# PSUM banks for the meta rows and the value bounds in the late in-projection jobs of a hybrid attention layer

## The chip, the cores and the metric

The kernel runs on one core of one Trainium2 chip. The metric is the device time of one execution, in microseconds (us), as the median of several runs.

## What is computed

One decoder layer. 16 learned meta tokens stand ahead of 1024 tokens of width 1024; everything is float32.

```
proj = rmsnorm(x) @ w_in      # c_q 256 | c_kv 128, k_r 32 | q_s 512 | k_s 512 | v_s 512 | indexer
o_mla = causal_block_attention(q_mla, k_mla, v_mla)     # q, k, v from rmsnorm(c_q) @ w_uq, rmsnorm(c_kv) @ w_ukv
score = where(causal, sum_h w_i * relu(q_i . k_i), -inf)
sel   = top_k(score, 256)                               # per query
o_dsa = softmax attention of rope(q_s) over rope(k_s)[sel], v_s[sel]
x = x + concat(o_mla, o_dsa) @ w_o
x = x + swiglu(rmsnorm(x)); out = rmsnorm(x), meta rows dropped
```

## The kernel before

**Products.** A float32 product is made of three products of split operands (`three`, L189 to L191: high by high, low by high, high by low). The sequence is cut into eight blocks t = 0..7 of 128 tokens (`NB`); the 16 meta rows stand apart, as `um`, with high and low part side by side, so that their products (`proj_m`, L307 and L308) are two and not three per slice of the contraction. The contraction has eight slices (`ND`).

**In-projection.** Its columns are cut into seven jobs (`run(i)`). A job loads its weights (`wraw`), splits them (`wh` by ACT at L181, `wl`), and makes for every block t a PSUM tile of 24 products, which `job` takes away (evacuates): the queries and keys of attention B through the ACT copy `st` (L516), the rotation on DVE (`rq`, L327 to L329) and a DMA to DRAM (`ks_x<-st`); the values by `v_parts`, an ACT product `vs` (L170) and a DVE one (L171), both scaled by `vsc`. After block t = 5 (`M_AT`) of a late job, `job_m` makes the meta rows; ACT copies their low half to `mlo` (L310) and DVE adds the high half to it (L311). Jobs 0 to 2 are the early ones (`EARLY`), and of the late ones job 3 (320 columns) holds queries and keys, job 4 keys, and jobs 5 and 6 values (256 columns each).

**The value bound.** Ahead of the tiles of jobs 5 and 6, `v_bound` bounds the values: ACT makes eight tiles `aw` = |wh| times the norm's gain (L574, two buffers), PE adds them up by products with ones (L575), and `v_scale` turns the sum into the power of two `vsc` on DVE (`vw`, L161 to L166). `mla_weights`, after job 3, has a bound of the same kind for attention A's values.

**What runs between.** `fill` puts steps of the top-k search for attention B's blocks between the tiles: on DVE a search round over two blocks' scores (L390, L390, L397, L398, L399, sixteen rounds) and after it the ranking of ties (L438 to L451), on ACT a search round over one block (`js` L375, then L376 and L378). After job 6 the parts of attention A follow (from L695), then attention B, the output projection and the FFN.

**Banks and order.** PSUM has eight banks, each a tile name `b0` to `b7` with one buffer. A ring is a string of bank digits taken in turn; a tile that gets a bank must wait until the last reader of that bank's earlier tile is done. Before the change the late jobs' blocks take the ring `ps_j` = 0,5,1,6,2,7,3, their meta rows the ring `ps_p` = 0,1,2, and the three bounds `ps_t` = 3,4. The program is written in the order of these loops; then a scheduler moves instructions within each engine's queue by its own timeline, and on the chip every engine runs its queue strictly in order.

Of the kernel before, what the change touches and what calls it, by code (L numbers as in the profile page):

```python
# [49 lines left out]
FILL = 1  # L50


PSI = "012", "34", "567", "0516273"
PSA = "01", "2345", "67"
PSB = "01", "2", "3", "4", "5", "67"
PSW = "45", "67", "23", "01"
# [3 lines left out]
EARLY, MLA_W, M_AT, XT_G, W_ENGS = 3, 3, 5, 2, "g"  # L60
# [38 lines left out]
def hybrid_layer(ctx, tc, a, out):  # L99
# [57 lines left out]
    def v_scale(pool, i, bound, rest):  # L157


        w = pool.tile([P, 4], F32, name="vw")  # L160
        V.reduce_max(w[:, 0:1], bound, axis=AX.X)  # L161
        V.tensor_scalar(w[:, 0:1], w[:, 0:1], 1e-25, None, op0=OP.max)
        wi, vi = w.bitcast(I32), vsc[i].bitcast(I32)
        V.tensor_scalar(wi[:, 1:2], wi[:, 0:1], 0x7F800000, None, op0=OP.bitwise_and)
        V.tensor_scalar(vi[:, 0:1], wi[:, 1:2], -1.0, float((268 - rest) << 23), op0=OP.mult, op1=OP.add)
        V.tensor_scalar(vi[:, 1:2], wi[:, 1:2], float((rest - 14) * (1 << 23)), None, op0=OP.add)  # L166

    def v_parts(h, l, src, i):
        n = src.shape[0]
        S.activation(h, src, AF.Copy, scale=vsc[i][:n, 0:1])  # L170
        V.scalar_tensor_tensor(l, src, vsc[i][:n, 0:1], h, op0=OP.mult, op1=OP.subtract)  # L171
# [23 lines left out]
    def ring(banks):  # L195

        turn = itertools.cycle(banks)
        return lambda: pp.tile([P, 512], F32, name=f"b{next(turn)}", bufs=1)
# [32 lines left out]


    with ExitStack() as es:
        ps_p, ps_t, ps_l, ps_j = (ring(x) for x in PSI)

        up = es.enter_context(tc.tile_pool(name="up", bufs=1))
        uH = up.tile([P, ND, T], F32R, name="uH")
# [11 lines left out]
        def load_chunk(c0, w, engs):  # L249

            res = []
            for d in range(ND):
                raw = wp.tile([P, 328], F32, name="wraw", bufs=3)
                ld(raw[:, :w], a["w_in"][0, d * P:(d + 1) * P, c0:c0 + w])
                h = wp.tile([P, 328], F32R, name="wh", bufs=2 * ND)
                l = wp.tile([P, 328], F32R, name="wl", bufs=2 * ND)
                split(h[:, :w], l[:, :w], raw[:, :w], engs[d % len(engs)])
                res.append((h, l))
            return res
# [39 lines left out]
                h, l = ws[d]  # L299
                three(o, uH[:, d, sl], uL[:, d, sl], h[:, :w], l[:, :w], d == 0, d == ND - 1)  # L300

        def proj_m(ws, w):

            o = ps_p()
            for d in range(ND):
                h, l = ws[d]
                PE.matmul(o[0:64, :w], um[:, d, :], h[:, :w], start=d == 0, stop=False)  # L307
                PE.matmul(o[0:64, :w], um[:, d, :], l[:, :w], start=False, stop=d == ND - 1)  # L308
            lo = ip.tile([NM, 328], F32, name="mlo", bufs=1)
            S.activation(lo[:, :w], o[32:32 + NM, :w], AF.Copy)  # L310
            V.tensor_add(lo[:, :w], o[0:NM, :w], lo[:, :w])  # L311
            return lo

        def rope(outs, src, cs, sn, shape, tag, eng=G, eng1=V):

            hf = shape[-1] // 2
            parts = shape[0]
            t1 = ip.tile([P] + list(shape[1:]), F32, name=tag + "1", bufs=2)[:parts]
            t2 = ip.tile([P] + list(shape[1:]), F32, name=tag + "2", bufs=2)[:parts]

            def bc(x):
                for _ in shape[1:-1]:
                    x = x[:, None]
                return x

            sh = list(shape[:-1]) + [hf]
            eng1.tensor_mul(t1, src, bc(cs).to_broadcast(list(shape)))  # L327
            V.tensor_mul(t2[..., 0:hf], src[..., hf:2 * hf], bc(sn[:, 0:hf]).to_broadcast(sh))
            V.tensor_mul(t2[..., hf:2 * hf], src[..., 0:hf], bc(sn[:, hf:2 * hf]).to_broadcast(sh))  # L329
            for o in outs:  # L330
                eng.tensor_add(o, t1, t2)
# [141 lines left out]
        m = proj_m(wk, 328)  # L473
# [33 lines left out]
        def latent(dst, src, n, g, parts=P):  # L507
            ss = ip.tile([P, 1], F32, name="ssc", bufs=3)[:parts]
            S.activation(act_junk()[:parts, :n], src, AF.Square, accum_out=ss)
            r = rstd(ip, ss, n, parts, "rsc")  # L510
            V.scalar_tensor_tensor(dst, src, r, g[:parts], op0=OP.mult, op1=OP.mult)

        def roped_heads(dx, rows, h0, src, cs, sn, scale=1.0, parts=P):
            n = src.shape[-1] // HD
            st = ip.tile([P, 5, HD], F32, name="st", bufs=3)[:parts, :n]
            S.activation(st, src.rearrange("p (h d) -> p h d", d=HD), AF.Copy, scale=scale)  # L516
            rope([st], st, cs, sn, [parts, n, HD], "rq")
            for i in range(2):
                ld(dx[rows, h0:h0 + n, i], st)

        def heads_of(c0, w):

            nq = max(0, min(w, O_KS - c0))
            res = [(0, (c0 - O_QS) // HD, nq, -HD ** -0.5)] if nq else []
            return res + ([(nq, (c0 + nq - O_KS) // HD, w - nq, 1.0)] if nq < w else [])
# [24 lines left out]
                if t == NB - 1:  # L550
                    ld(v_x[1][:, 4 * g:4 * g + 4, :, 1:], vs)

        def job_m(c0, w, ws):
            if c0 < O_CKV or O_CKV < c0 < O_KS - 64:
                return
            m = proj_m(ws, w)
            if c0 == O_CKV:
                latent(cm[:, 0:KVR], m[:, 0:KVR], KVR, gq[:, QR:], NM)
                rope([cm[:, KVR:160]], m[:, KVR:160], ropem[:, 128:160], ropem[:, 160:192], [NM, RD], "rr", V)
            elif c0 < O_VS:  # L560
                c, h, n, _ = heads_of(c0, w)[-1]
                roped_heads(ks_m, slice(0, NM), h, m[:, c:c + n], ropem[:, 0:64], ropem[:, 64:128], 1.0, NM)
            else:
                g = (c0 - O_VS) // 256
                mv = vsp.tile([NM, 4, 2, HD], F16, name="mv")
                v_parts(mv[:, :, 0], mv[:, :, 1], m[:, :w].rearrange("p (h d) -> p h d", d=HD), 1 + g)
                ld(v_x[1][PAD:, 4 * g:4 * g + 4, :, 0], mv)

        def v_bound(c0, w, ws):

            pb = ps_t()
            for d, (h, _) in enumerate(ws):
                aw = vsp.tile([P, 256], F32R, name="aw", bufs=2)
                S.activation(aw[:, :w], h[:, :w], AF.Abs, scale=gcol[:, d:d + 1])  # L574
                PE.matmul(pb[:, :w], ones, aw[:, :w], start=d == 0, stop=d == ND - 1)  # L575
            v_scale(vsp, 1 + (c0 - O_VS) // 256, pb[:, :w], 5)
# [4 lines left out]
        def run(i):  # L581
            c0, w = jobs[i]
            ws = nxt.pop()
            if i + 1 < len(jobs):
                nxt.append(load_chunk(*jobs[i + 1], ENG_W))
            if c0 >= O_VS:
                v_bound(c0, w, ws)
            for t in range(NB):
                po = (ps_p if i < EARLY else ps_j)()
                proj(po[:, :w], t, ws, w)  # L590
                job(c0, w, t, po)
                fill(FILL)
                if t == (NB - 1 if i < EARLY else M_AT):
                    job_m(c0, w, ws)

        flush()
        for i in range(EARLY):
            run(i)
# [21 lines left out]
        def mla_weights():  # L620
            def v8(t):
                return t.rearrange("p (h d) -> p h d", h=8)

            def raw(src):
                x = wp.tile([P, 328], F32, name="wraw", bufs=3)
                ld(x[:, 0:256], src)
                return x[:, 0:256]

            for c in range(4):
                x = raw(a["w_ukv"][0, :, c * 256:(c + 1) * 256]).rearrange("p (h t d) -> p h t d", h=2, t=2)  # L630
                hs = slice(2 * c, 2 * c + 2)
                split(v8(wkH)[:, hs], v8(wkL)[:, hs], x[:, :, 0], G)
                split(v8(wvH)[:, hs], v8(wvL)[:, hs], x[:, :, 1], G)
            for k in range(2):
                for c in range(3):
                    cs = slice(c * 256, (c + 1) * 256)
                    split(wqH[:, k, cs], wqL[:, k, cs], raw(a["w_uq"][0, k * P:(k + 1) * P, cs]), G)
            pb = ps_t()
            for c in range(2):
                cs = slice(c * 256, (c + 1) * 256)  # L640
                aw = vsp.tile([P, 256], F32R, name="aw", bufs=2)
                S.activation(aw, wvH[:, cs], AF.Abs, scale=gcol[:, ND:])
                PE.matmul(pb[:, cs], ones, aw, start=True, stop=True)
            v_scale(vsp, 0, pb, 4)
# [18 lines left out]
    ps_s, ps_t, ps_o = (ring(x) for x in PSA)  # L663
# [513 lines left out]
    ps_s, ps_t, ps_o, ps_g, ps_u, ps_y = (ring(x) for x in PSB)  # L1177
# [75 lines left out]
```

## Time and profile before

| | |
|---|---|
| median of 3 runs | 1524.23 us (1519.41 to 1525.39) |
| profiled execution | 1528.41 us, its span 1526.6 us |
| mean granted TensorE clock | 0.981 of full speed |
| busy share of the span | PE 94%, PE weight load 87%, DVE 59%, ACT 55%, POOL 52% |

The shares are means over the whole span. Times below are positions in the span of the profiled execution, which is 0.27% longer than the median; the late jobs lie between about 200 and 327 us.

### The profile page before, as it was taken

To read this page: it belongs to the slowest core of one execution; us is meant where nothing else is said; L and a number is where in the kernel's file an instruction comes from. 1 tells how busy PE (TensorE), PEld (TensorE's weight loads), DVE (VectorE), ACT (ScalarE), POOL (GpSimd) and SP (SyncE) were. 2 spreads that over 40 slices of the span, in tenths; PEclk is the share of its full clock that TensorE was granted. 3 is DMA by queue.
4 is the path that set the end of the run, shared out by engine and by line. 5 is a ranking of instruction groups with operands and counts; after the bars stand their busy time and mean duration, and the time that the engine had idled before them with its cause. 6 is when DMAs were issued, how large, how long until landed. Compare 5 with 4: busy or idle time off the path is not lost. (4 is left out here: it accounts for less than half of the span.)

```text
span 1526.6 us, 29766 instructions
## 1 busy us (share of the span) xinstructions
PE 1434.4 (94%) x10584; PEld 1332.2 (87%) x10584; DVE 907.2 (59%) x2447; ACT 846.6 (55%) x2038; POOL 796.2 (52%) x1121
## 2 busy tenths in 40 slices
PE   6999998999989899899899999999999999999997
PEld 5999998888778788788798899888899999999996
DVE  6879989948886876966866666415422222213225
ACT  5666678797889889797544453435412122122223
POOL 2663555212405678786887888531634344343342
PEclk9999999999999799999999999999999999999999
DMA  6123355224434787587799997431322222222221
GB/s 180 50 52 85 86 136 125 47 88 143 125 103 107 163 187 171 138 182 148 177 212 200 204 210 172 138 108 39 125 82 84 67 85 65 74 83 70 83 70 69
DMA packets 353732, 180.71 MB, mean 118 GB/s; under 512 B 196560, under 2 KB 341344, under 8 KB 353584
## 3 DMA queue, kind: packets, MB, share of 16 engines
q1 hardware_dynamic: 353584, 178.82, 46.7%
q8 instruction: 83, 1.36, 0.4%
q14 instruction: 65, 0.53, 0.1%
HBM read 120.77 MB, written 21.30 MB: 93 GB/s over the span
## 5 line engine op out<-in xcount | busy, mean ns | idle before, releaser
L184 POOL TENSOR_TENSOR wL<-raw,wH 128x256 fp32r<-128x256 f32 x528 | 399.1, 787 | 303.0 <-ACT wH L181 293.3
L181 ACT ACTIVATE wH<-raw 128x1024 fp32r<-128x1024 f32 x132 | 139.7, 1058 | 263.2 <-PE b L191 96.4
L189 PE MATMUL b<-ub,wH 128*128 128x384 f32 (+1 forms) x704 | 218.6, 311 | 1.2 <-ACT wH L181 1.2
L190 PE MATMUL b<-ub,wH 128*128 128x384 f32 (+1 forms) x704 | 218.5, 311 | 0.0
L191 PE MATMUL b<-ub,wL 128*128 128x384 f32 (+1 forms) x704 | 217.8, 310 | 0.0
L814 POOL TENSOR_TENSOR hl<-pd,hl 128x260 f16<-128x260 f32 (+5 forms) x256 | 168.4, 686 | 72.6 <-ACT hl L810 39.6
L189 PE MATMUL b<-wh,uH 128*128 128x256 f32 (+3 forms) x568 | 169.1, 298 | 5.3 <-DVE mlo L311 2.6
L191 PE MATMUL b<-wh,uL 128*128 128x256 f32 (+3 forms) x568 | 168.5, 297 | 0.0
L190 PE MATMUL b<-wl,uH 128*128 128x256 f32 (+3 forms) x568 | 168.1, 296 | 0.1
L1107 DVE TENSOR_TENSOR oh<-b,oh 128x512 f32<-128x512 f32 x146 | 99.2, 686 | 74.5 <-PE b L191 74.1
L189 PE MATMUL b<-wH,hH 128*128 128x512 f32 x352 | 140.5, 399 | 1.8 <-DVE oh L1107 0.8
L190 PE MATMUL b<-wL,hH 128*128 128x512 f32 x352 | 138.7, 394 | 0.0
L191 PE MATMUL b<-wH,hL 128*128 128x512 f32 x352 | 136.0, 393 | 0.4 <-DVE hL L186 0.4
L189 PEld LDWEIGHTS b<-ub,wH 128*128 128x128 f32 x704 | 132.8, 189 | 3.1 <-ACT wH L181 1.5
L190 PEld LDWEIGHTS b<-ub,wH 128*128 128x128 f32 x704 | 132.2, 188 | 1.2
L191 PEld LDWEIGHTS b<-ub,wL 128*128 128x128 f32 x704 | 132.1, 188 | 1.1
L189 PE MATMUL b<-ua,wH 128*128 128x384 f32 x352 | 122.0, 347 | 4.0 <-ACT wH L181 4.0
L375 ACT ACTIVATE js<-sc,bs 128x528 bf16<-128x528 int16 (+7 forms) x128 | 120.8, 944 | 4.1 <-DVE sc L430 1.7
L191 PE MATMUL b<-ua,wL 128*128 128x384 f32 x352 | 121.0, 344 | 0.0
L190 PE MATMUL b<-ua,wH 128*128 128x384 f32 x352 | 120.9, 343 | 0.0
L1093 DVE SCALAR_TENSOR_TENSOR sg<-sg,b 128x384 f32<-128x384 f32 x66 | 33.5, 508 | 144.5 <-ACT sg L1092 144.5
L189 PEld LDWEIGHTS b<-wh,uH 128*128 128x128 f32 x568 | 108.6, 191 | 7.4 <-DVE mlo L311 3.4
(326 smaller groups left out, 4026.6 us busy)
## 6 DMA issues: line engine op xcount, KB each, us to landing
raw<-in_w_gate SPq DMA_DIRECT2D x44, 512.0 KB, 4.1
raw<-in_w_up SPq DMA_DIRECT2D x44, 512.0 KB, 4.0
raw<-in_w_down SPq DMA_DIRECT2D x44, 512.0 KB, 3.6
wor<-in_w_o SPq DMA_DIRECT2D x64, 128.0 KB, 2.6
wraw<-in_w_in SPq DMA_DIRECT2D x40, 128.0 KB, 2.3
vh<-v_x SPq DMA_DIRECT2D x16, 288.0 KB, 3.8
xt<-in_x SPq DMA_DIRECT2D x8, 512.0 KB, 4.3
ks_x<-st SPq DMA_DIRECT2D x32, 128.0 KB, 2.2
```

The costliest lines, as they stand in the source:

```text
L181: S.activation(h, src, AF.Copy)
L184: G.tensor_sub(l[:, c], src[:, c], h[:, c])
L189: PE.matmul(o, lh, rh, start=first, stop=False)
L190: PE.matmul(o, lh, rl, start=False, stop=False)
L191: PE.matmul(o, ll, rh, start=False, stop=last)
L375: S.activation(act_junk()[:, :n_keys(b)], y[b], AF.Sign, bias=cols[0], accum_out=cnt)
L814: G.tensor_sub(pl_[:, c], pb[:, c], ph[:, c])
L1093: V.scalar_tensor_tensor(sg, sg, 1.0, pg, op0=OP.add, op1=OP.mult)
L1107: V.tensor_add(oh[t][:, cs], po, oh[t][:, cs])
```

## The change

Late jobs now take their meta rows' bank from the same ring as their blocks, as one more slot between t = 5 and t = 6. All three bounds take a ring of their own with the single bank 4, which in this stage only `ps_t` holds besides.

```
-PSI = "012", "34", "567", "0516273"
+PSI = "012", "34", "567", "0516273", "4"
...
-        ps_p, ps_t, ps_l, ps_j = (ring(x) for x in PSI)
+        ps_p, ps_t, ps_l, ps_j, ps_b = (ring(x) for x in PSI)
...
-        def proj_m(ws, w):
+        def proj_m(ws, w, ps=ps_p):
 
-            o = ps_p()
+            o = ps()
...
         def v_bound(c0, w, ws):
 
-            pb = ps_t()
+            pb = ps_b()
...
+            ps = ps_p if i < EARLY else ps_j
             for t in range(NB):
-                po = (ps_p if i < EARLY else ps_j)()
+                po = ps()
...
-                    job_m(c0, w, ws)
+                    job_m(c0, w, ws, ps)
...
-            pb = ps_t()              # in mla_weights
+            pb = ps_b()
```

No engine gets an instruction more or less. The banks of the late jobs become these (blocks t = 0 to 5, then meta rows m, then t = 6, 7):

| job | before | after |
|---|---|---|
| 3 | 0 5 1 6 2 7, m 2, 3 0 | 0 5 1 6 2 7, m 3, 0 5 |
| 4 | 5 1 6 2 7 3, m 0, 0 5 | 1 6 2 7 3 0, m 5, 1 6 |
| 5 | bound 3; 1 6 2 7 3 0, m 1, 5 1 | bound 4; 2 7 3 0 5 1, m 6, 2 7 |
| 6 | bound 4; 6 2 7 3 0 5, m 2, 1 6 | bound 4; 3 0 5 1 6 2, m 7, 3 0 |

The scheduler's order changes with them, on all engines from job 3 on to the end of attention B. In the rows of the order, a name ends in the number of its buffer, and `b3_4420` is a tile in bank 3.

PE, where the meta rows of job 3 (`3574`) begin, before; `3604` is job 3's block t = 6:

```order
L189 MATMUL b3_3604<-wh_2771,uH_109 128x320
L190 MATMUL b3_3604<-wl_2772,uH_109 128x320
L191 MATMUL b3_3604<-wh_2771,uL_110 128x320
L307 MATMUL b2_3574<-wh_2750,um_111 64x320
L308 MATMUL b2_3574<-wl_2751,um_111 64x320
```

And after, where `3507` is its block t = 5:

```order
L189 MATMUL b7_3507<-wh_2799,uH_109 128x320
L190 MATMUL b7_3507<-wl_2800,uH_109 128x320
L191 MATMUL b7_3507<-wh_2799,uL_110 128x320
L308 MATMUL b3_3574<-wl_2751,um_111 64x320
L307 MATMUL b3_3574<-wh_2757,um_111 64x320
```

The meta rows moved ahead of block 6: before they stand behind its 24 products.

PE, around the bound of job 5 (`4420`), before; `4311` is job 4's block 7, `4250` its block 6, and `4451` and `4505` are job 5's blocks 0 and 1:

```order
L190 MATMUL b5_4311<-wl_3153,uH_109 128x256
L191 MATMUL b5_4311<-wh_3152,uL_110 128x256
L575 MATMUL b3_4420<-aw_4421,ones_83 128x256
L575 MATMUL b3_4420<-aw_4424,ones_83 128x256
L189 MATMUL b1_4451<-wh_3806,uH_109 128x256
...
L190 MATMUL b0_4250<-wl_3153,uH_109 128x256
L191 MATMUL b0_4250<-wh_3152,uL_110 128x256
L575 MATMUL b3_4420<-aw_4427,ones_83 128x256
L189 MATMUL b1_4451<-wh_3812,uH_109 128x256
L190 MATMUL b1_4451<-wl_3813,uH_109 128x256
L575 MATMUL b3_4420<-aw_4430,ones_83 128x256
L191 MATMUL b1_4451<-wh_3812,uL_110 128x256
```

And after:

```order
L190 MATMUL b6_4311<-wl_3153,uH_109 128x256
L191 MATMUL b6_4311<-wh_3152,uL_110 128x256
L575 MATMUL b4_4420<-aw_4421,ones_83 128x256
L575 MATMUL b4_4420<-aw_4424,ones_83 128x256
L189 MATMUL b2_4451<-wh_3806,uH_109 128x256
...
L190 MATMUL b2_4451<-wl_3849,uH_109 128x256
L191 MATMUL b2_4451<-wh_3848,uL_110 128x256
L189 MATMUL b7_4505<-wh_3806,uH_109 128x256
L190 MATMUL b7_4505<-wl_3807,uH_109 128x256
L191 MATMUL b7_4505<-wh_3806,uL_110 128x256
L189 MATMUL b7_4505<-wh_3812,uH_109 128x256
L575 MATMUL b4_4420<-aw_4427,ones_83 128x256
```

Job 4's block 6 no longer stands behind the first two products of the bound; the third product of the bound stands behind a whole block and four products of the next one, and it waits for the third `aw`.

DVE, where the bound of job 5 is read (`vw` L161), before; `jk` with L390 is a round of the search:

```order
L390 TENSOR_SCALAR jk_4353,bs1_3201<-sc1_102,bs1_3201 128x272
L390 TENSOR_SCALAR jk_4355,bs1_3201<-sc2_103,bs1_3201 128x400
L397 TENSOR_TENSOR bs1_3201<-bs1_3201 128x2
L398 TENSOR_SCALAR bs1_3201<-bs1_3201 128x2
L161 TENSOR_REDUCE vw_4445<-b3_4420 128x1
L399 SCALAR_TENSOR_TENSOR bs1_3201<-bs1_3201 128x2
L162 TENSOR_SCALAR vw_4445<-vw_4445 128x1
L390 TENSOR_SCALAR jk_4479,bs1_3201<-sc1_102,bs1_3201 128x272
L390 TENSOR_SCALAR jk_4481,bs1_3201<-sc2_103,bs1_3201 128x400
L164 TENSOR_SCALAR vw_4445<-vw_4445 128x1
L397 TENSOR_TENSOR bs1_3201<-bs1_3201 128x2
L165 TENSOR_SCALAR vsc1_81<-vw_4445 128x1
```

And after:

```order
L390 TENSOR_SCALAR jk_4488,bs1_3201<-sc2_103,bs1_3201 128x400
L397 TENSOR_TENSOR bs1_3201<-bs1_3201 128x2
L398 TENSOR_SCALAR bs1_3201<-bs1_3201 128x2
L399 SCALAR_TENSOR_TENSOR bs1_3201<-bs1_3201 128x2
L161 TENSOR_REDUCE vw_4445<-b4_4420 128x1
L438 TENSOR_SCALAR jk_4532,bs1_3201<-sc1_102,bs1_3201 128x272
L441 TENSOR_SCALAR jk_4535<-sc1_102,bs1_3201 128x272
L162 TENSOR_SCALAR vw_4445<-vw_4445 128x1
L439 TENSOR_TENSOR bs1_3201<-bs1_3201 128x1
L442 SCALAR_TENSOR_TENSOR jk_4535<-sc1_102,bs1_3201,jk_4535 128x272
L164 TENSOR_SCALAR vw_4445<-vw_4445 128x1
L444 SCALAR_TENSOR_TENSOR jk_4536<-jk_4535 128x272
```

The rounds with `jk_4479` and `jk_4486`, which stood behind the reading of the bound, stand ahead of it, and the ranking (L438 to L444) begins ahead of `vsc1_81` (L165).

ACT, where the evacuation of job 5's blocks begins (`vs` L170), before; `js` L375 with L376 and L378 is a round of ACT's search:

```order
L378 ACTIVATE bs4_4147<-bs4_4147 128x1
L574 ACTIVATE aw_4828<-wh_4374,gcol_85 128x256
L375 ACTIVATE js_4360,bs4_4147<-sc4_105,bs4_4147 128x656
L574 ACTIVATE aw_4831<-wh_4380,gcol_85 128x256
L181 ACTIVATE wh_4416<-wraw_4414 128x256
L376 ACTIVATE bs4_4147<-bs4_4147,th4_4148 128x1
L378 ACTIVATE bs4_4147<-bs4_4147 128x1
L170 ACTIVATE vs_4476<-b1_4451,vsc1_81 128x4x64
L170 ACTIVATE vs_4476<-b6_4505,vsc1_81 128x4x64
```

And after:

```order
L376 ACTIVATE bs4_4147<-bs4_4147,th4_4148 128x1
L378 ACTIVATE bs4_4147<-bs4_4147 128x1
L574 ACTIVATE aw_4831<-wh_4380,gcol_85 128x256
L375 ACTIVATE js_4368,bs4_4147<-sc4_105,bs4_4147 128x656
L376 ACTIVATE bs4_4147<-bs4_4147,th4_4148 128x1
L378 ACTIVATE bs4_4147<-bs4_4147 128x1
L375 ACTIVATE js_4493,bs4_4147<-sc4_105,bs4_4147 128x656
L170 ACTIVATE vs_4476<-b2_4451,vsc1_81 128x4x64
L170 ACTIVATE vs_4476<-b7_4505,vsc1_81 128x4x64
```

The round `js_4368` stood behind block 0's evacuation and stands ahead of it, as does the next one's first step `js_4493`.

## Rows read from the trace of the kernel before

**Rows 1.** The profile page: busy time of each engine with its share of the span and its number of instructions, and the TensorE clock granted in 40 equal slices, in tenths of full speed (9 is 90% or more).
```profile
PE 1434.4 (94%) x10584; PEld 1332.2 (87%) x10584; DVE 907.2 (59%) x2447; ACT 846.6 (55%) x2038; POOL 796.2 (52%) x1121
...
PEclk9999999999999799999999999999999999999999
```

**Rows 2.** What PE waited for between 225 and 345 us: engine, waiting line, what it waited for; us in total, times, longest.
```profile
PE b L307 <- ACT st L516: 4.7, 1, 4.7
PE b L575 <- ACT st L516: 2.8, 1, 2.8
PE b L189 <- DVE mlo L311: 2.4, 2, 1.4
PE b L189 <- ACT cqH L181: 1.6, 1, 1.6
PE b L189 <- DVE vw L161: 1.0, 1, 1.0
```

**Rows 3.** The five bank waits on PE's timeline: start, us, engine, line, operation, out<-in, form; in brackets the idle time before it and what ended that.
```profile
233.00 0.53 PE L307 MATMUL b<-wh,um 128*64 128x320 f32 x1 [4.74 <-ACT st L516]
...
266.71 0.58 PE L575 MATMUL b<-aw,ones 128*128 128x256 f32 x1 [2.79 <-ACT st L516]
...
269.55 0.58 PE L189 MATMUL b<-wh,uH 128*128 128x256 f32 x1 [1.40 <-DVE mlo L311]
...
287.01 0.39 PE L189 MATMUL b<-wh,uH 128*128 128x256 f32 x1 [1.05 <-DVE vw L161]
...
299.83 0.38 PE L189 MATMUL b<-wh,uH 128*128 128x256 f32 x1 [1.03 <-DVE mlo L311]
```

**Rows 4.** Busy time in stretches: stretch and its length; then busy us (and instructions) of PE, PE's weight load, DVE, ACT, POOL; granted clock as a share, DMA share, GB/s.
```profile
226.00:275.00 49.00, 40.07 (x291) 38.82 (x290) 45.13 (x167) 40.18 (x126) 26.73 (x39) 0.90 0.51 119
...
275.00:302.00 27.00, 24.92 (x210) 24.51 (x209) 26.01 (x93) 21.22 (x61) 5.14 (x7) 1.00 0.18 42
...
300.00:325.00 25.00, 25.00 (x214) 25.00 (x214) 8.88 (x26) 22.95 (x63) 0.40 (x2) 1.00 0.13 44
...
302.00:340.00 38.00, 36.22 (x276) 34.85 (x275) 16.81 (x55) 35.13 (x101) 7.15 (x23) 1.00 0.28 89
...
228.00:259.00 31.00, 26.27 (x200) 25.51 (x200) 30.15 (x125) 23.90 (x76) 18.55 (x27) 0.94 0.56 132
...
263.00:302.00 39.00, 32.73 (x252) 31.82 (x252) 37.66 (x122) 31.73 (x92) 10.03 (x14) 0.91 0.23 53
...
340.00:460.00 120.00, 108.20 (x1043) 93.37 (x1042) 105.38 (x319) 96.47 (x297) 33.20 (x54) 0.99 0.40 119
...
460.00:1000.00 540.00, 506.65 (x4200) 458.76 (x4200) 362.97 (x915) 356.58 (x787) 401.62 (x565) 0.97 0.77 172
```

**Rows 5.** DVE's timeline, columns as in rows 3.
```profile
260.93 0.43 DVE L327 TENSOR_TENSOR rq<-st,rope 128x256 f32<-128x256 f32 x1 [1.35 <-ACT st L516]
...
263.12 0.76 DVE L438 TENSOR_SCALAR_CACHE_REDUCE jk<-sc,bs 128x528 bf16<-128x528 uint16 x1 [1.36 <-POOL bs L383]
...
283.05 0.50 DVE L390 TENSOR_SCALAR_CACHE_REDUCE jk<-sc,bs 128x272 bf16<-128x272 uint16 x1
...
284.74 0.50 DVE L390 TENSOR_SCALAR_CACHE_REDUCE jk<-sc,bs 128x272 bf16<-128x272 uint16 x1
...
286.55 0.41 DVE L161 TENSOR_REDUCE vw<-b 128x1 f32<-128x256 f32 x1
...
288.23 0.15 DVE L165 TENSOR_SCALAR vsc<-vw 128x1 int32<-128x1 int32 x1
...
291.63 0.49 DVE L438 TENSOR_SCALAR_CACHE_REDUCE jk<-sc,bs 128x272 bf16<-128x272 uint16 x1
...
293.67 0.50 DVE L445 SCALAR_TENSOR_TENSOR jk<-jk,bs 128x272 bf16<-128x272 f16 x1
...
301.95 0.20 DVE L451 TENSOR_TENSOR sc<-sc,cbias 128x128 bf16<-128x128 bf16 x1
```

**Rows 6.** ACT's timeline, columns as in rows 3.
```profile
237.00 0.22 ACT L516 ACTIVATE st<-b 128x64 f32<-128x64 f32 x1 [2.16 <-DMA ks_x<-st]
...
271.38 0.49 ACT L574 ACTIVATE aw<-wh,gcol 128x256 fp32r<-128x256 f32 x1
...
282.94 0.42 ACT L181 ACTIVATE wh<-wraw 128x256 fp32r<-128x256 f32 x1 [2.77 <-DMA wraw<-in_w_in]
...
288.41 0.47 ACT L170 ACTIVATE vs<-b,vsc 128x256 f16<-128x256 f32 x1 [2.09 <-DVE vsc L165]
...
293.19 0.83 ACT L375 ACTIVATE js<-sc,bs 128x656 bf16<-128x656 int16 x1
...
294.81 0.84 ACT L375 ACTIVATE js<-sc,bs 128x656 bf16<-128x656 int16 x1
...
295.65 0.45 ACT L170 ACTIVATE vs<-b,vsc 128x256 f16<-128x256 f32 x1
```

**Rows 7.** PE's timeline, the first product of attention A.
```profile
327.10 0.23 PE L695 MATMUL b<-ident,cm 16*128 16x16 f32 x1
```

**Rows 8.** What PE waited for between 340 and 1000 us: us in total, times, longest.
```profile
PE b L783 <- DVE sm L785: 12.1, 12, 3.0
```

More of the change, by code (lines that the diff above doesn't have):

```diff
@@ L551, in job, with job_m @@
                     ld(v_x[1][:, 4 * g:4 * g + 4, :, 1:], vs)
-        def job_m(c0, w, ws):
+        def job_m(c0, w, ws, ps):
             if c0 < O_CKV or O_CKV < c0 < O_KS - 64:
                 return
-            m = proj_m(ws, w)
+            m = proj_m(ws, w, ps)
             if c0 == O_CKV:
```

## The prediction

> **What bounds the kernel now.** I read the shares first, then the waits of PE in the stretch that the change touches, then who is late there.
>
> Over the whole span PE is busy 94% and no other engine is above 59%; the granted clock is full in all but one of the 40 slices [rows 1]. So a microsecond that PE stands idle is worth a microsecond, but only where nothing else sets the end of the stretch. The list of PE's waits between 225 and 345 us names the places that the change addresses [rows 2]: the meta rows of job 3 wait 4.74 us for bank 2, the bound of job 5 waits 2.79 us for bank 3 (both end with ACT's copy `st`), a block waits 1.40 us and another 1.03 us for `mlo`, that is for a bank that meta rows have taken, and one 1.05 us for `vw`, a bank that a bound has taken [rows 3]. The wait for `cqH` is not a bank and is left alone. The five are 4.74 + 2.79 + 1.40 + 1.05 + 1.03 = 11.0 us.
>
> Then the stretches, because a mean over 1526 us says little on 100 of them [rows 4]. From 226 to 275 us PE is busy 40.07 of 49 us, its weight load 38.82, ACT 40.18, and DVE 45.13. From 275 to 302 us PE has 24.92 of 27, DVE 26.01. Finer: DVE has 30.15 of 31 us between 228 and 259, and 37.66 of 39 between 263 and 302. Between them it waits twice, 1.35 us for an `st` and 1.36 us for a small step of the search on POOL [rows 5]. So in the late jobs DVE works without a break, and PE waits because banks come free as fast as ACT and DVE empty them. Banks are taken one after another, and each is given back by those two engines; a PE that waits less at one bank meets the next one that is still full. This is the reading on which my forecast rests.
>
> From 302 us on it turns: DVE has 16.81 us of work in 38, PE 36.22 and ACT 35.13 [rows 4]. Here PE and ACT set the pace until attention A's first product at 327.10 us [rows 7].
>
> **The change part by part.** Nothing is added or removed, so the sum is one of waits alone.
>
> *The meta rows of jobs 3 and 4 ahead of block 6.* In the new order they follow block 5 at once, in a bank last read by an earlier job (3 and 5). The 4.74 us of job 3 go, and for PE that is the whole price, upper bound 4.74, lower bound 0 if the new bank is as full. The same holds for `mlo`: block 6 and block 7 get banks that blocks 0 and 1 of the same job have left, not the one of the meta rows, so 1.40 + 1.03 us go.
>
> *The bound of job 5 in bank 4.* Its first product waits for no `st` now, since the last reader of bank 4 is the bound of attention A's values: 2.79 us go. But the order of its products changes. The third stands behind job 5's block 0 and four products of block 1, and needs the third `aw`, which ACT makes at 271.38 us [rows 6] and no earlier in its own order. When is PE there? Before, it was done with block 7 of job 4 at 266.71 - 2.79 = 263.9 us. Take off the 4.74 us of job 3, add block 6 of job 4, which now lies ahead (24 products), and the 28 products of job 5. A product of 256 columns takes 25.00 / 214 = 0.117 us in a stretch where PE is full [rows 4], so 52 of them are 6.1 us. That makes 263.9 - 4.7 + 6.1 = 265.3 us, and a wait until about 271.8: some 6.5 us, `PE L575 <- ACT aw`. The removed waits ran into a new one.
>
> *The search ahead of the bound's reading.* On DVE two more rounds of the search and the first part of the ranking stand ahead of `vsc`. A round is 284.74 - 283.05 = 1.69 us; the ranking from L438 to L444 is 293.67 - 291.63 = 2.04 us [rows 5]. Of one of these two rounds the greater part lay ahead of `vsc` already (it is at 288.23, and `vw` at 286.55), so I add one round, two small steps of 0.16 to 0.2 each, and the ranking: 1.69 + 0.36 + 2.04 = 4.1 us. `vsc` would come at 288.23 + 4.1 = 292.3 us, less what DVE has gained. On ACT the first evacuation of job 5 waits for `vsc` (2.09 us now, at 288.41) [rows 6]. In the new order it has two rounds more ahead of it and a first step: a round is 294.81 - 293.19 = 1.62 us and the step 295.65 - 294.81 = 0.84, together 4.1 us. So what DVE delays is filled on ACT with rounds that it would have had to run afterwards; the two are equal, and I count the exchange as nothing. If ACT's rounds were not there to cover it, it would cost up to 4.1 us; that is the lower bound of this step. PE feels it as a wait of block 6 of job 5 for block 0's bank: after the third `aw` it has 20 + 96 + 16 products left ahead of that block, 132 x 0.117 = 15.4 us, so it is there at about 287.5 and the bank comes at about 292 to 293.5: some 5 us.
>
> *Sum for PE's waits.* Away: 4.74 + 2.79 + 1.40 + 1.05 + 1.03 = 11.0. New: 6.5 + 5 = 11.5. They change places.
>
> *What remains is what DVE and ACT gain.* DVE is the engine without a break, so the late jobs end earlier only by the part of its two waits that goes, between 0 and 1.35 + 1.36 = 2.71 us. The first is for an `st` of a block that PE now makes earlier; the second is for POOL, which nothing moves. I take 1.0 us, nearest to the first. ACT's waits for DMAs, 2.16 us for the write of keys and 2.77 us for weights [rows 6], are not shortened by a bank. After 302 us PE and ACT carry this 1.0 us one to one to 327.10 [rows 7].
>
> *Behind the late jobs* the work in attention A and B is the same but interleaved otherwise. PE's idle time there is 120 - 108.20 + 540 - 506.65 = 45.2 us between 340 and 1000 us [rows 4]. I have no row that says which way it goes; a tenth of it, 4.5 us, in either direction is an allowance and no calculation.
>
> So the profiled execution would be 1528.4 - 1.0 = 1527.4 us, and since the median stands 4.2 us below the profiled execution, the median **1523.2 us**. The forecast's own range is 1517 to 1529: 2.7 + 4.5 us down, rounded, and 4.5 + 1 up.
>
> **A rule weighed.** By the rows DVE bounds the stretch 226 to 275 us (45.13 of 49 us against 38.82 of the weight load) [rows 4]. The Trainium skill (Perfetto Trace Analysis, Identifying the Most-Contended Engine) judges by occupancy, for TensorE by the weight load's busy share, and would have the busiest engine optimized first; over the whole span that is PE with 87% against DVE's 59% [rows 1], and the five waits would be worth their full 11.0 us. The same page (Optimization Strategy) says that the most contended engine may change over time, and read by stretch it names DVE here, as the rows do. Which of the two readings holds is what rival A is about.
>
> **Rivals.**
>
> *A, the waits come back (faster).* If PE bounds the late jobs after all, because the searches on DVE and ACT are filler that may slip past 302 us, where DVE has over 21 us to spare, then the 11.0 us return. With fewer waits the clock may stay up too: it is granted at 0.90 from 226 to 275 us [rows 4], which is 49 x 0.10 = 4.9 us of columns. Together 15.9 us, a median of about 1508. For it: PE is busy 25.00 of 25 us from 300 to 325 us, so an earlier arrival there would not be lost to DVE. Against it: the queues are in order, and `vsc`, which job 5's evacuation needs, stands behind the filler in DVE's queue, further behind than before. Chance 0.22, with the cases in which about half of it comes back.
>
> *B, the later interleaving is worse (slower).* The scheduler's order shifts through attention B. PE's largest wait there is for `sm`, the reduction on DVE behind the scores, 12 waits of 12.1 us, about 1.0 us each [rows 8]. Eight more such waits would give 1523.2 + 8 = 1531, and that is the point from which it counts as slower. For it: DVE is busy 105.38 of 120 us between 340 and 460 us [rows 4], so an unlucky order there has nowhere to go. Against it: the same searches are done by then in both orders, and the instructions are the same. Chance 0.17.
>
> *C, the change does nothing at all.* The bank waits and the `vsc` delay cancel and the later order holds: 1524. It is the forecast's neighbour and lies in its range.
>
> **How the numbers follow.** 0.5% is 7.6 us, about what a measurement of this kernel can tell from no change. Forecast and C: 0.61. A: 0.22, nearly all of it faster by over 0.5% (below 1516.6). B: 0.17 above 1531.8. The forecast's own range does not hold 8 in 10, so the range reaches to the near halves of both rivals: **1510 to 1532.5**.
>
> **What the changed profile would show.** Right: the waits of L307 and L575 for `st` and of L189 for `mlo` are gone; in their place L575 waits for `aw` some 6.5 us at about 265 to 272, and a block of job 5 about 5 us near 290 for an evacuation; `vsc` at 291 to 292; ACT's first `vs` waits for it; DVE without a break from 263 to 302; the first product of attention A at 326 (324.4 to 327.1). Wrong by A: that product at 320 or earlier and the clock at full in 226 to 275. Wrong by B: that product where I put it, and more waits for `sm` or other idle time of PE behind 340 us. The forecast also falls if DVE has idle time in the late jobs in the new order, since then it is not what bounds them.

## The result

The change makes the kernel slower: median 1544.2 us (1543.83 to 1546.06, 4 runs) against 1524.8 us for the kernel before (1519.41 to 1525.39), ratio 1.0134, 95% interval 1.0105 to 1.0162. The profiled execution is 1544.31 us against 1528.41. The forecast was 1523.2 us, with a range of 1510 to 1532.5.

The page of the changed kernel, the lines that answer to [rows 1]:

```profile
PE 1442.3 (94%) x10584; PEld 1337.4 (87%) x10584; DVE 909.7 (59%) x2447; ACT 846.0 (55%) x2038; POOL 795.9 (52%) x1121
...
PEclk9999999899999899999999999899999999999999
```

All engines do the same instructions as before. PE's busy time grew by 1442.3 - 1434.4 = 7.9 us, and its idle time from 1526.6 - 1434.4 = 92.2 to 1542.5 - 1442.3 = 100.2 us. So of the 15.9 us of the profiled execution half is idle time, and half is the same products taking longer, which fits the lower granted clock (0.974 on average against 0.981).

**The late jobs went much as forecast.** What PE waited for between 225 and 345 us, the longest first, against [rows 2] (us in total, times, longest):

```profile
PE b L575 <- ACT aw L574: 12.1, 3, 10.4
PE b L189 <- ACT cqH L181: 2.7, 1, 2.7
PE b L189 <- DVE kL L186: 0.6, 1, 0.6
...
PE b L189 <- DVE vs L171: 0.3, 1, 0.3
```

The places that explain it, on the timeline (PE, ACT, DVE and PE again):

```profile
274.50 0.58 PE L575 MATMUL b<-aw,ones 128*128 128x256 f32 x1 [10.38 <-ACT aw L574]
...
273.95 0.49 ACT L574 ACTIVATE aw<-wh,gcol 128x256 fp32r<-128x256 f32 x1
...
292.57 0.13 DVE L165 TENSOR_SCALAR vsc<-vw 128x1 int32<-128x1 int32 x1
...
326.93 0.23 PE L696 MATMUL b<-ident,cm 16*128 16x16 f32 x1
```

The waits of L307 and L575 for `st`, of L189 for `mlo` and for `vw` are gone, and L575 waits 10.38 us for the third `aw` instead, because ACT makes it at 273.95 us. In sum PE waits 12.1 us there instead of 11.0. `vsc` comes at 292.57 us. The first product of attention A (the line has one number more in this kernel) starts at 326.93 us, against 327.10 in [rows 7]. That 0.2 us is less than one kernel differs from the next: in the seven profiled executions with both new rings and the search's steps in the late jobs it starts between 326.1 and 328.5 us, in the nine with both old ones between 325.4 and 328.7, and both means are 327.0.

Busy time in the same stretches as [rows 4]:

```profile
226.00:275.00 49.00, 38.62 (x310) 38.25 (x309) 46.41 (x168) 40.61 (x127) 26.08 (x40) 0.94 0.53 123
275.00:302.00 27.00, 25.49 (x198) 25.06 (x197) 25.78 (x94) 20.69 (x59) 5.04 (x7) 0.92 0.16 36
302.00:340.00 38.00, 34.17 (x255) 33.12 (x255) 14.64 (x51) 34.33 (x99) 5.03 (x17) 0.96 0.28 89
...
228.00:259.00 31.00, 31.00 (x252) 30.95 (x251) 30.00 (x122) 24.71 (x80) 18.15 (x27) 1.00 0.57 131
...
263.00:302.00 39.00, 27.11 (x208) 26.48 (x207) 37.71 (x120) 31.07 (x89) 9.69 (x13) 0.87 0.23 54
```

DVE is as full as before (30.00 of 31 us, 37.71 of 39) while PE's waits and its clock changed places inside the stretch: none from 228 to 259, more from 263 to 302.

**The loss lies in attention B.** For the products that PE does from 740 us to the end of attention B and a little beyond, almost the same number in both kernels, the kernel before takes 261 us,

```profile
740.00:1001.00 261.00, 249.42 (x2102) 227.04 (x2101) 163.09 (x389) 118.33 (x246) 202.66 (x281) 0.99 0.82 187
```

and the changed kernel 276.6:

```profile
740.00:1016.60 276.60, 257.50 (x2097) 231.35 (x2096) 163.28 (x392) 123.94 (x264) 205.01 (x282) 0.96 0.77 174
```

Counted by its products, PE in the changed kernel is 1.9 us ahead of the kernel before at the 5500th (756 us in the kernel before), 12.2 us behind it at the 6000th (818 us), and 15.8 us behind from the 8000th on. So most of the loss falls between 756 and 818 us.

The mask of block 7, the last of the selection masks, is finished by L451 on DVE. Before:

```profile
757.42 0.28 DVE L451 TENSOR_TENSOR sc<-sc,cbias 128x128 bf16<-128x128 bf16 x1
```

and in the changed kernel:

```profile
768.53 0.63 DVE L451 TENSOR_TENSOR sc<-sc,cbias 128x128 bf16<-128x128 bf16 x1
```

It is 11.1 us later. Around this moment the stretches look so before (columns as in rows 4):

```profile
740.00:757.00 17.00, 15.50 (x144) 14.06 (x142) 16.51 (x20) 5.62 (x12) 13.13 (x15) 1.00 0.84 185
757.00:777.00 20.00, 18.81 (x144) 17.62 (x145) 14.59 (x42) 10.23 (x20) 18.63 (x27) 1.00 0.76 201
777.00:800.00 23.00, 23.00 (x212) 21.07 (x209) 16.45 (x43) 12.54 (x26) 19.12 (x28) 1.00 0.96 204
```

and so in the changed kernel:

```profile
740.00:757.00 17.00, 17.00 (x150) 15.65 (x149) 8.34 (x18) 13.75 (x31) 9.77 (x16) 1.00 0.87 183
757.00:777.00 20.00, 15.86 (x84) 14.15 (x81) 13.80 (x17) 4.38 (x7) 16.26 (x15) 0.83 0.29 90
777.00:800.00 23.00, 22.64 (x158) 20.52 (x158) 15.80 (x40) 11.66 (x23) 18.95 (x27) 1.00 0.66 163
```

Between 757 and 777 us PE does 84 products instead of 144, at a granted clock of 0.83, and ACT is busy 4.38 us instead of 10.23. Of the 84, 61 follow each other between the last values product (757.5 us) and the next scores (776.5 us). All 61 are products of the FFN, which stand in PE's queue as filler, and they wait for their own weights, as the first two rows (PE) show; the third row (ACT) shows that ACT, which splits these weights, had waited 6.30 us for their DMA. The fourth row (PE) is from the end of attention B, where the last filler has run (978.8 us) and PE waits for the transposed `pT`:

```profile
766.67 0.45 PE L189 MATMUL b<-ua,wH 128*128 128x384 f32 x1 [2.60 <-ACT wH L181]
...
768.26 0.69 PE L191 MATMUL b<-ua,wL 128*128 128x384 f32 x1 [0.97 <-POOL wL L184]
...
765.57 1.06 ACT L181 ACTIVATE wH<-raw 128x1024 fp32r<-128x1024 f32 x1 [6.30 <-DMA raw<-in_w_gate]
...
981.77 0.20 PE L824 MATMUL b<-vh,pT 128*128 128x64 f16 x1 [2.92 <-DMA pT<-hl]
```

The mask alone does not fill this stretch. On DVE two reductions behind the scores (`pd`, L786) follow the mask at once, and then DVE waits for PE's filler:

```profile
769.09 0.51 DVE L786 CUSTOM_DVE_ANT_0 pd<-b,sc 128x348 f32<-128x348 f32 x1
...
769.64 0.58 DVE L786 CUSTOM_DVE_ANT_0 pd<-b,sc,sm 128x348 f32<-128x348 f32 x1
...
775.58 1.29 DVE L1108 TENSOR_TENSOR oh<-b,oh 128x512 f32<-128x512 f32 x2 [5.35 <-PE b L191]
777.02 0.58 DVE L786 CUSTOM_DVE_ANT_0 pd<-b,sc,sm 128x344 f32<-128x344 f32 x1
```

The mask is finished at 769.2 us and these two reductions at 770.2, but the next scores start at 776.5. In between PE works through the filler that stands ahead of them in its queue.

The order of the two kernels has this in it: between two products of attention B, PE's queue of the changed kernel holds one stretch of 61 filler products; behind the start of the FFN filler up to the end of attention B the longest in the kernel before has 37 (from 582 to 589 us), and none above 25 lies near the mask. On ACT, the 49th of the 64 search rounds over blocks 6 and 7 is instruction 1193 of the queue in the changed kernel and 1167 in the kernel before.

### The profile page after: what moved, and what is told of

Same layout as the page of the kernel before. It is cut to its first block, busy times and chain, and to the rows that moved or that the text cites. A ratio compares the mean times of both kernels' runs of the same rounds, so it can differ in the third digit from the quotient of the medians.

```text
span 1542.5 us, 29747 instructions
## 1 busy us (share of the span) xinstructions
PE 1442.3 (94%) x10584; PEld 1337.4 (87%) x10584; DVE 909.7 (59%) x2447; ACT 846.0 (55%) x2038; POOL 795.9 (52%) x1121
## 4 chain that ended last, share of the span: by engine, by line
PE 43%; DVE 14%; POOL 9%; DMA 8%; ACT 8%; issue 7%; SPq 1%; DVEq 0%; ACTq 0%; POOLq 0%
PE b L189 12%; PE b L191 12%; PE b L190 12%; POOL wL L184 5%; PE b L784 3%; POOL hl L815 3%; DVE jk L390 2%; DMA pT<-hl 2%; ACT js L375 2%; DMA wor<-in_w_o 1%; DMA raw<-in_w_gate 1%; DMA raw<-in_w_up 1%; DVE bs L399 1%; DVE oh L1108 1%; ACT wH L181 1%
## 5 line engine op out<-in xcount | busy, mean ns | idle before, releaser
L189 PE MATMUL b<-ub,wH 128*128 128x384 f32 (+1 forms) x704 | 218.7, 311 | 1.1 <-ACT wH L181 1.1
L189 PE MATMUL b<-wh,uH 128*128 128x256 f32 (+3 forms) x568 | 168.8, 297 | 2.0 <-DVE rq L329 1.0
L189 PE MATMUL b<-wH,hH 128*128 128x512 f32 x352 | 140.8, 400 | 2.3 <-ACT hH L181 1.4
L189 PEld LDWEIGHTS b<-ub,wH 128*128 128x128 f32 x704 | 132.8, 189 | 3.0 <-ACT wH L181 1.3
L189 PE MATMUL b<-ua,wH 128*128 128x384 f32 x352 | 123.6, 351 | 5.9 <-ACT wH L181 5.9
L375 ACT ACTIVATE js<-sc,bs 128x528 bf16<-128x528 int16 (+7 forms) x128 | 120.9, 944 | 5.0 <-DVE sc L430 2.6
L189 PEld LDWEIGHTS b<-wh,uH 128*128 128x128 f32 x568 | 108.5, 191 | 3.6 <-ACT kiH L181 1.2
```

Source lines behind the costliest of these rows:

```text
L189: PE.matmul(o, lh, rh, start=first, stop=False)
L375: S.activation(act_junk()[:, :n_keys(b)], y[b], AF.Sign, bias=cols[0], accum_out=cnt)
```

## The experiments

**Old and new order behind job 6 (e1, e2).** In both kernels an instruction has the same number in the written program. The part written behind job 6 (attention A and B, output projection, FFN) is put in a given order on all five queues by edges between neighbours that make no wait, and the rest is left to the scheduler. e1 is the changed kernel with the order of the kernel before, e2 the kernel before with the order of the changed one.

```
+def pin(tc, first):
+    have = {i.name: i for i in tc.nc.cur_bb.bb.instructions}
...
+            if n <= first or i is None:
+                continue
+            if last is not None:
+                tc.add_manual_dep(i, last, mybir.DependencyInfo(mybir.DependencyClass.NoSync, mybir.DependencyReason.DATA), reason="pin")
+            last = i.name
```

> The changed kernel with its own order up to the end of job 6, but everything written behind job 6 (attention A, attention B, output projection, FFN) issued on all five queues in the order of the kernel before. Theory 'later order': the 19 us of the change come from the order behind job 6, so this kernel is back at 1522 to 1530 us, and the first product of attention A still stands at about 327 us. Rival 'banks and late jobs': the cost comes with the new banks or the state in which the late jobs leave the engines, so it stays at 1538 to 1546 us.

> The mirror image: the kernel before with its banks and its order up to the end of job 6, but everything written behind job 6 issued in the order of the changed kernel. Theory 'later order': 1538 to 1546 us, with none of the bank changes made. Rival 'banks and late jobs': 1520 to 1530 us.

e1: 1527.68 us, ratio 1.0011 (0.9988 to 1.0034). e2: 1543.14 us, ratio 1.0114 (1.0087 to 1.0140). Both came as the theory said. The banks and the late jobs cost nothing that can be measured; the order behind job 6 carries 1.1 of the 1.3%. In e1 PE waits in the late jobs as in the changed kernel:

```profile
PE b L575 <- ACT aw L574: 11.6, 3, 10.5
PE b L189 <- DVE vs L171: 0.4, 1, 0.4
```


**One half of the change at a time (e3, e4).** e3 gives only the meta rows their new bank, e4 only the bounds; each edit is against the changed kernel, e3's first.

```
-            pb = ps_b()
+            pb = ps_t()
```
```
-                    job_m(c0, w, ws, ps)
+                    job_m(c0, w, ws, ps_p)
```

> The meta rows of the late jobs take the jobs' ring, the bounds keep banks 3 and 4. The order behind job 6 is that of the kernel before but for 8 products. Theory 'later order': 1520 to 1530 us, and the wait of L307 for st (4.7 us) is gone without the time following it. Rival 'banks': the meta rows make most of the change's front differences, so most of the 19 us are there, 1535 us or more.

> The bounds take bank 4, the meta rows keep the early ring. On every engine the order is that of the kernel before; only two banks differ. Theory 'later order': 1519 to 1527 us; the 2.79 us wait of L575 for st goes, and if DVE sets the pace of the late jobs the first product of attention A moves by less than 1 us. Rival 'banks': slower by several us.

e3: 1529.76 us, ratio 1.0027 (1.0005 to 1.0050). e4: 1528.47 us, ratio 1.0007 (0.9988 to 1.0026). Each half leaves the order behind job 6 as it was (e4 wholly, e3 but for 8 products of PE); only both together turn it over. In e4 the wait of L575 for `st` is gone, and what PE waited for in the late jobs is this:

```profile
PE b L189 <- DVE mlo L311: 5.9, 2, 3.0
PE b L307 <- ACT st L516: 5.2, 1, 5.2
```

That is 11.1 us again. e3 waits 11.0 us in sum. e4 is 1.5 us over its expected range. Attention A's first product starts at 329.2 us, 2.1 us later than in the kernel before where less than 1 us was expected; that is about the spread given above. Here bank waits moved; they did not go.

**The pace of the search (e5, e6).**

```
-TOPK_B = [([[5]], False, 2), ([[6], [7]], True, 3)]
+TOPK_B = [([[5]], False, 2), ([[6], [7]], True, 6)]
```

> The changed kernel with six instead of three steps of the search over blocks 6 and 7 per step of attention B. Theory 'search chain': the loss is the late mask of block 7 (its ranking ends at 769 us instead of 758), for which attention B and so PE's queue wait; with the search twice as fast the mask is ready before 730 us, the stretch of filler alone on PE around 757 to 777 us is gone and the time falls to 1518 to 1532 us. Rival 'chance of the order': where the fillers stand is what costs, the search is only one of many things that moved; then the mask comes earlier and the time stays anywhere, 1535 us or more as likely as not.

> The kernel before with the same six steps. Theory 'search chain': before, PE is not idle around the mask of block 7 (757 us), so an earlier mask is worth little: 1515 to 1526 us, and e5 comes within 6 us of this kernel, where the two differ by 19 us at three steps. Rival 'chance of the order': the two differ by 10 us or more in either direction.

Both missed: 1562.22 us (1.0249, 1.0208 to 1.0290) and 1548.5 us (1.0152, 1.0114 to 1.0191). Block 7's mask came at 770 and 752 us instead of 769 and 758, but block 5's, which DVE searches, at 795 and 777 instead of 653 and 643 us. It became the last mask, so an early last mask was not tested.

**No steps of the search in the late jobs (e7, e8).**

```
-                fill(FILL)
+                fill(FILL if i < EARLY else 0)
```

> The changed kernel without any step of the search in jobs 3 to 6; the steps run later, in attention A, so only the arrival at attention A's first product is to be read. Theory 'DVE and ACT set the pace of the late jobs': without the search's rounds both have time, the bank waits fall to under 4 us in sum, and the arrival is 8 us or more earlier than 327 us, the same as in e8 within 2 us. Rival 'the banks set it' (rival A of the prediction): this kernel arrives 5 us or more ahead of e8.

> The kernel before, likewise without steps of the search in jobs 3 to 6. Theory 'DVE and ACT set the pace': arrival at attention A's first product 8 us or more earlier than 327 us, within 2 us of e7. Rival 'the banks set it': the old banks still wait some 10 us in sum and the arrival is 5 us or more behind e7.

This did not do what it was made for. The scheduler puts the rounds, written later now, into the same gaps: DVE is busy 45.84 and 45.73 of the 49 us from 226, about as in [rows 4] (45.13), so the claim that DVE and ACT set the pace of the late jobs was not tested. Attention A's first product starts at 326.1 and 327.2 us, not 8 us earlier. As one execution each, 1543.61 and 1518.76 us, they repeat the difference of the two later orders.

**A shorter search (e9, e10) and another division of blocks (e11, e12).**

```
-                for k in range(15, -1, -1):
+                for k in range(3 if b == 7 and first else 15, -1, -1):
```
```
-TOPK_B = [([[5]], False, 2), ([[6], [7]], True, 3)]
+TOPK_B = [([[7]], False, 2), ([[5], [6]], True, 3)]
```

> The changed kernel with 4 of the 16 rounds of the second search over block 7's scores; the other 12 are left out, so the choice of keys among equal high halves is not made in full for that block. Theory 'last mask': in the eight kernels run so far the time follows the moment at which the last block's mask is ready (752 us and 1519 up to 795 us and 1562, about 1 us per us). 12 rounds of about 4.6 us make that moment some 50 us earlier, attention B does not wait for it any more, and the time falls to 1500 to 1522 us, within 7 us of e10. Rival 'chance of the order': the time stays with the order of the changed kernel, 1535 us or more, and differs from e10 by 12 us or more.

> The kernel before with the same 12 rounds left out (the choice among equal high halves is not made in full for block 7). Theory 'last mask': 1500 to 1522 us, as e9. Rival 'chance of the order': 1525 us or any other time, and no nearer to e9 than the two kernels are at full length.

> The changed kernel with the searches dealt out otherwise: DVE searches block 7 and ACT blocks 5 and 6, so ACT's 64 rounds are over 784 and 912 scores in place of 912 and 1040, nothing is left out. Theory 'last mask': a round of ACT is 0.2 to 0.3 us shorter, and the last mask (now block 6, with a shorter ranking) comes some 10 us earlier if the order keeps its pace; the time follows it one to one: last mask at about 757 us, 1525 to 1538 us. Rival: no relation between mask and time.

> The kernel before with the same exchange of blocks 5 and 7. Theory 'last mask': last mask at 743 to 752 us and a time of 1508 to 1522 us, which beats both kernels. Rival: 1525 us or more with the mask as early as that.

e9: 1526.4 us, ratio 1.0009 (0.9994 to 1.0024); e10: 1521.15 us, 0.9964 (0.9946 to 0.9981). With the mask early the changed kernel gains 18 us and the kernel before 4, and they stand 5 us apart instead of 19. e9 is 4 us above what was expected. e9 and e10 are not pinned, so the scheduler also moved other rows in them. e11: 1534.01 us, 1.0055 (1.0040 to 1.0070), inside its range; e12: 1529.17 us, 1.0026 (1.0009 to 1.0043), a miss, since its last mask moved by only 2 us.

**Only the search's rows moved (e13 to e16).** ACT's queue behind job 6 is pinned as in e1, with the 188 rows of the search over blocks 6 and 7 at other places among the rest; the other queues follow as the scheduler decides.

> The changed kernel in which, behind job 6, ACT's queue is given: the other rows in the changed kernel's order, and the 188 rows of the search over blocks 6 and 7 at the places (counted in other rows ahead of them) where the kernel before has them. The other queues are free to follow. Theory 'last mask': the mask of block 7 is back at 755 to 760 us and the time at 1522 to 1532 us. Rival 'other rows of the order': 1538 us or more.

> The mirror image: the kernel before with only the 188 search rows at the changed kernel's places in ACT's queue, 8 to 26 rows further behind. Theory 'last mask': mask at 766 to 770 us and 1537 to 1546 us. Rival 'other rows': 1520 to 1530 us.

> The kernel before with the same 188 rows up to 30 places further ahead in ACT's queue. Theory 'last mask': the mask comes some 20 us earlier, and because the two values products around it stand 13 us apart in the kernel before, where they stand 8 apart without a late mask (e10), a small gain is left: 1512 to 1524 us. Rival: the rounds ahead hold up the rest of ACT's queue and it is slower than 1526 us.

> The changed kernel with the search rows up to 30 places ahead of where the kernel before has them. Theory 'last mask': within 6 us of e15. Rival 'other rows': it stays 10 us or more above e15.

1566.6 us (1.0269), 1554.15 us (1.0194), 1566.3 us (1.0272), 1587.39 us (1.0406), all slower than both kernels. e14 went in the expected direction and too far, the others against the theory. In e13 the mask did not come back: it came at 778.6 us, as in e14. In e15 the mask came at 749.8 us, 8 us earlier than before, and the kernel was 40 us slower. From 460 to 640 us, in e15:

```profile
460.00:640.00 180.00, 148.02 (x1141) 132.51 (x1141) 123.74 (x335) 144.49 (x339) 106.11 (x146) 0.89 0.57 128
```

and in the kernel before:

```profile
460.00:640.00 180.00, 164.50 (x1359) 148.45 (x1359) 134.04 (x362) 154.70 (x361) 123.27 (x175) 0.94 0.70 157
```

PE does 218 products less there, and one of its waits in e15, which the kernel before hardly has (0.2 us from 480 to 1001 us), is for ACT's copy of attention B's results (`oh`):

```profile
PE b L824 <- ACT oh L827: 7.0, 2, 4.8
```

That fits rounds forced ahead which hold up the rest of ACT's queue. No run pinned ACT's queue alone with its rows left in place, so what the moved rows cost and what the freed other queues cost is not parted.

An early mask is not enough, and a table of mask against time over the kernels up to e12 (us; the third column is the longest time between two products of values from 690 to 960 us, the fourth the profiled execution) is no law either. e11 has an earlier mask than the kernel before and no long stretch, and is slower:

| kernel | last mask | longest stretch without values | profiled |
|---|---|---|---|
| e10 | 708.5 | 8.0 | 1514.5 |
| e9 | 733.1 | 9.3 | 1519.6 |
| e11 | 752.0 | 9.1 | 1533.8 |
| e8 | 752.3 | 13.2 | 1518.8 |
| e4 | 754.0 | 13.2 | 1524.9 |
| e1 | 755.2 | 13.2 | 1528.8 |
| e12 | 755.4 | 11.1 | 1529.1 |
| e3 | 756.7 | 13.2 | 1530.9 |
| before | 757.7 | 13.2 | 1528.4 |
| e2 | 768.3 | 33.7 | 1542.5 |
| e7 | 768.2 | 33.3 | 1543.6 |
| after | 769.2 | 34.6 | 1544.3 |
| e6 | 776.7 | 56.9 | 1550.2 |
| e5 | 795.2 | 63.6 | 1557.2 |

**The same order, one piece of work longer (e17, e18).** Behind job 6 all five queues are pinned to the kernel's own order, and four repeated scans are put into the ranking of block 7.

```
                 V.tensor_tensor_scan(rk, e, e, 0.0, OP.add, OP.bypass)
+                for _ in range(4 if b == 7 else 0):
+                    more.append(int(V.tensor_tensor_scan(rk, e, e, 0.0, OP.add, OP.bypass).ins.name[2:]))
```

> The kernel before, all queues in its own order, with the scan of block 7's ranking (L444, 2.75 us) made five times instead of once: four rows more on DVE, 11 us, directly ahead of block 7's mask, which is so about as late as in the changed kernel (769 us). Theory 'the late mask costs': attention B stands at that mask, so the time grows by 8 to 14 us, to 1533 to 1539 us. Rival 'the mask has slack, it is the rest of the new order': 3 us or less.

> The kernel of e10 (second search of block 7 with 4 of 16 rounds, the choice among equal high halves not made in full), all queues in its own order, with the same four scans more. There the mask is ready at 708 us and attention B does not wait for it. Theory 'the late mask costs': 4 us or less above e10, that is 1518 to 1526 us. If it is the 11 us of DVE work that cost: 8 us or more above e10.

e17: 1537.04 us, ratio 1.0056 (1.0034 to 1.0078), inside its range. e18: 1530.99 us, 1.0027 (1.0011 to 1.0042), some 10 us above e10, a miss: the control lost as much. The masks came at 765.4 us in e17 and, 14 us later than in e10, at 722.5 in e18. What PE waited for in e17 between 740 and 765 us (us in total, times, longest):

```profile
PE b L931 <- DVE qH L941: 11.4, 1, 11.4
```

and DVE's queue there (`qH` is the split of the next head's queries):

```profile
748.22 10.40 DVE L446 TENSOR_TENSOR_SCAN jk<-jk 128x1040 f16<-128x1040 bf16 x4
758.66 1.58 DVE L447 SCALAR_TENSOR_TENSOR jk<-jk,bs 128x1040 bf16<-128x1040 f16 x1
760.27 0.29 DVE L941 TENSOR_TENSOR qH<-b,qH 64x128 fp32r<-64x128 f32 x1
```

PE does not wait for the mask here but for `qH`, which stands behind the scans in DVE's queue. Product by product, PE is 1.7 us ahead of the kernel before at 349.5 us, 9.3 us behind it at 758.2 and 8.6 us at 968.6. So 10.4 us of scans made the kernel later, more or less one to one. e17's time came out as the theory said, but not by its way.

## Why the prediction was wrong

*The waits of the late jobs* were right in kind and place for the larger one. The new wait of L575 for `aw` was put at 6.5 us and measured 10.38, because `aw` came 2.6 us later than in [rows 6] and PE 1.2 us earlier than worked out. The wait of about 5 us near 290 us was 0.3 (`vs` L171): PE left the wait for `aw` 2.7 us later than worked out, and its granted clock from 275 to 302 us was 0.92, by estimate another 27 x 0.08 = 2.2 us. So the sums, 11.5 forecast and 12.1 measured, agree by luck: two misses cancel. `vsc` was expected at 291 to 292 us and stood at 292.57. The 1.0 us of gain was 0.2, which is no gain within the spread of this point: DVE's wait for `st` of [rows 5] is gone, and DVE stayed full without getting ahead.

*Rival A* is excluded by the same rows: L307 no longer waits, the granted clock from 228 to 259 us is full, and nothing of it arrives at attention A. That DVE's and ACT's work is the reason remains the reading of the rows; e7 and e8, made to test it, left that work in place. By the Trainium skill (Perfetto Trace Analysis, Optimization Strategy) the most contended engine may change over time. The trace agrees: from 263 to 302 us DVE is busy 37.71 of 39 us and PE's weight load 26.48, while over the whole span it is 59% and 87%.

*The step that failed* is the one on what lies behind the late jobs. Its term was an allowance of 4.5 us in either direction for an order that "is interleaved otherwise"; it measured +16 us in the profiled execution, and e1 and e2 show that this order alone carries it. The allowance was a tenth of PE's idle time there, which is no bound: half of the loss is longer busy time, which idle time does not contain. The prediction also held against a worse order that "the same searches are done by then". They are not: in the kernel before, the last mask comes at 757.42 us, in the middle of attention B, and rounds of the search behind it are among what the new order moved back. And it read the clock as full in all but one of the slices of [rows 1], where a 9 is 90% or more; [rows 4] has 0.97 from 460 to 1000 us.

*Rival B* named the right side and the right stage, attention B, and the wrong price and mechanism, 1531 us by waits for `sm`. Only the second half of its sign, other idle time of PE behind 340 us, came true. PE's waits for `sm` got no dearer; before, from 480 to 1001 us:

```profile
PE b L783 <- DVE sm L785: 11.6, 11, 3.0
```

and in the changed kernel, from 482.7 to 1016.6 us:

```profile
PE b L784 <- DVE sm L786: 7.0, 13, 1.5
```

Its point of decision, eight more such waits, was never reached.

**What is shown, and what is open.** Shown: the loss comes with the order behind job 6 and is not in the banks, and it lies in attention B behind 740 us, most of it around the last mask, where filler stands alone on PE for some 19 us. Supported: that the late search makes it, since with a shorter search the changed kernel gains 18 us and the kernel before 4. Against this as the whole cause stands e11, 8 us slower than the kernel before without a late mask. Open: whether the mask itself, DVE's queue behind its ranking (e18 could not part them) or the place of the filler in PE's queue is what holds attention B, and why the two halves of the change turn the order over only together. No run moved the 61 filler products alone. e8, one execution of 1518.76 us beside seven of the kernel before from 1520.43 up, may be faster than both kernels; it was not timed further, and no version that does the whole work was shown to beat the kernel before.

## What to carry to other kernels

Where a scheduler orders the program, a change of two buffers can change everything behind it: compare the orders to the very end, and look there for long runs of filler between two pieces of the critical stream, and for a serial chain (here 64 search rounds) whose rounds move back. To see whether a change or the order that came with it costs, run each kernel in the other's order, on all queues. The waits for buffers were worth nothing here, where another engine was busy without a break; they turned up again at the next buffer. Moving the search's rows in ACT's queue by hand, with the other queues free, cost 2 to 4%.

## What the runs showed of the hardware

The granted clock, 2.4 or 1.2 GHz, was 0.83 of full speed on average from 757 to 777 us in the changed kernel, where PE had gaps of 2.60 and 0.97 us, and 1.00 in the stretches on both sides. Over the whole execution 8.0 us of added idle time came with 7.9 us of added time for the same products. The two need not go together: e17, with one long wait of 11.4 us, has 10.2 us more idle time than the kernel before and 1.8 us less busy time (1432.6 us for the same 10584 products).
